# One-hots of a gather emitted a step earlier, scattered rows added one block at a time, the last turns moved ahead

## Chip, cores and metric

The kernel runs on one core of a Trainium2 chip. The time is device microseconds of one execution of the whole program; the figure compared is the median over runs. The core has five engines with queues of their own: PE (TensorE, matrix products), DVE (VectorE), ACT (ScalarE), POOL (GpSimd) and SP (SyncE, which here only issues transfers). An engine works off its own queue in order.

## What is computed

The reference is a two-layer backbone over 256 latent tokens of width 1024. Layer 0 ends in a dense SwiGLU, layer 1 in a mixture of eight experts of which each token takes two. The change touches only what follows the mixer of layer 1:

```python
h = modulate(rmsnorm(x), shift, scale)
logits = h @ moe_router                       # 256 x 8
top, idx = top2(logits); comb = softmax(top)  # two experts per token
for e in range(8):                            # E_FF = 3584
    y_e = (silu(h_e @ w1[e]) * (h_e @ w3[e])) @ w2[e]
x = x + gate * sum_e comb_e * y_e
out = rmsnorm(x) * final_norm_g
```

Every weight is float32; an expert has 3 x 14 MB, all eight have 336 MB.

## The kernel before

The program has a first part (mixers and the dense FFN, to about 820 us) and then `moe`, which fills the rest. `moe` reads the expert weights in **units** of 1 MB: an expert's 3584 hidden columns are cut in `EFF_CH` = 7 chunks, and a chunk has six units, two each of w1, w3 and w2. That is 8 x 7 x 6 = 336 units. All are issued by SP (L119) in the order in which the program takes them, into ten recycled buffers (nine called `raw`, one `mraw`); beside these, 8 halves called `first`, an `early` buffer and three buffers called `once` are filled before the experts begin. A recycled buffer is loaded again when its last reader is done.

**Heavy and light.** After routing, `by_load` ranks the experts by how many tokens chose them. Three are heavy (up to 128 tokens each), five are light (up to 64). A heavy unit is split into two parts by ACT (`CAST`, L145) and DVE (the remainder, L146), and PE does three products per tile (L176, L181, L182; twelve matmuls a unit). A light unit is used as it lies (L1157 for w1 and w3, L1184 for w2), with two 64-column halves side by side. `moe_turn` and `light_turn` transpose the hidden activations (L1117, L1170) and copy them to `G` (L1120, L1121) or `GL` (L1172) for the w2 product.

**Steps.** A step is one chunk of one expert. The list begins with `self.lead` = 4 light chunks of expert 0 and then mixes heavy and light chunks at an even rate. The order of instructions on PE, ACT and DVE in `moe` is pinned to the order in which the code is written. Small work of other kinds is hung between the units through callbacks: `aside` in `moe_first` (four places a heavy step, one behind each w1 or w3 unit), `heavy_aside` and `light_aside`. `look_ahead` splits the next planned unit.

**Gather.** `gather` forms the rows of one heavy and one light expert. `one_hot` (L1047) builds 0/1 matrices `P` and `Q` from each token's position; then for each of eight 128-column blocks of the width four matmuls (L1058, `sm <- P,H`) pick the rows, and DVE (L1062, L1064) and ACT (L1063 into `XE`, L1066 into `XL`) modulate and store them. `turned` transposes `P` and `Q` (L1073) and ACT casts them (L1074) for the way back. It is a generator that yields behind each block; `side` is the one under way, and `run(side, n)` moves it n yields on. `begin` does expert 0's gather, routing weights, `by_load`, and the gather of experts 1 and 4. Later gathers are started behind certain light steps (`more`).

**Scatter.** When an expert is done, `scatter` or `light_scatter` scales its output into two parts `Y`, and four times `put` multiplies them by the transposed one-hots (L1208, L1209) and adds the result, times the token's weight, to the residual (DVE, L1211). These generators lie in `late`; `puts()` runs them to the end.

**Router.** `last_proj.finish(t)` makes the logits of one of two token tiles; `route` then ranks both (L957 to L963), forms the combination weights with an exponential on ACT (L977), and the positions (L989 to L995). POOL does the two H2 subtractions of tile 1 (L1596).

Of the kernel before, what the change touches and what calls it, by code (L numbers as in the profile page):

```python
# [49 lines left out]
class Net:  # L50
    def __init__(self, tc, d, dump=None):
# [18 lines left out]
        self.hact, self.hpool = (1,), (1,)  # L70
# [873 lines left out]

    def route(self):
# [3 lines left out]
        lg, sel, oh1, oh2 = self.lg, T("sel"), T("oh1"), T("oh2")  # L949
        big = E.tile([128, 2, 2, 8, 8], F32, tag="P", name="big", bufs=1)  # L950
        gt, ge = (big[:, i] for i in range(2))
        selb = E.tile([128, 2, 8], BF16, name="selb")
        rank = T("rank")
        for t in range(2):
            mine = lg[:, t, :, None].to_broadcast([128, 8, 8])
            other = lg[:, t, None, :].to_broadcast([128, 8, 8])
            V.tensor_tensor(ge[:, t], other, mine, op=ALU.is_equal)  # L957
            V.tensor_tensor(ge[:, t], ge[:, t], self.low, op=ALU.mult)
            V.tensor_tensor(gt[:, t], other, mine, op=ALU.is_gt)
            V.tensor_tensor(gt[:, t], gt[:, t], ge[:, t], op=ALU.add)  # L960
            V.tensor_reduce(rank[:, t], gt[:, t], axis=AX.X, op=ALU.add)
            V.tensor_scalar(selb[:, t], rank[:, t], 1.5, None, op0=ALU.is_lt)
            V.tensor_scalar(sel[:, t], rank[:, t], 1.5, None, op0=ALU.is_lt)  # L963
# [32 lines left out]
        self.comb, self.sel, self.pos, self.tmp = comb, sel, pos, tmp  # L996
        self.dbg("pos", pos)

    def by_load(self):
# [31 lines left out]
        self.placed.append(table("combS", self.comb))  # L1031
# [18 lines left out]
    def gather(self, P, XE=None, XL=None):  # L1050
# [3 lines left out]
        for k in range(8):  # L1054
# [10 lines left out]
            if XL is not None:  # L1065
                nc.scalar.activation(XL[:, k], pg[:, o:], AF.Identity, bias=sh, scale=A)  # L1066
# [15 lines left out]
    def moe_first(self, src, XE, c, aside=lambda n: None):  # L1082
# [3 lines left out]
        for n, name in enumerate(("m_w1", "m_w3")):  # L1086
            ps = self.bank(tag="mm")
            for kh in range(2):
# [8 lines left out]
                self.look_ahead()  # L1097
                aside(2 * n + kh)
# [89 lines left out]
    def scatter(self, PT, y, cmb):  # L1188
# [24 lines left out]
    def light_scatter(self, PT, y, cmb):  # L1213
# [16 lines left out]
    def moe(self):  # L1230
# [3 lines left out]
        def tables(i):  # L1234
            tabs = (self.pos, self.sel, self.comb) if i == 0 else self.placed
            return [a[:, :2, i:i + 1] for a in tabs]

        def light(i, P):
# [4 lines left out]
            pos, sel, _ = tables(i)  # L1243
# [6 lines left out]
        def heavy(i, P):  # L1250
            pos, sel, _ = tables(i)
# [9 lines left out]
        def gather(i, j):  # L1261
# [4 lines left out]
            Q = light(j, P)  # L1266
            yield from self.gather(P[:, :, 0 if i else 128:192], XE.get(i), XE[j])
# [19 lines left out]
        run(side, 9)  # L1287
# [22 lines left out]

        def second(kind, **kw):

            while todo[kind] and todo[kind][0] in G:
# [21 lines left out]
        for m, (i, c) in enumerate(steps):  # L1335
            kind = big(i)
            if i == 0 and c == 4:
# [9 lines left out]
            def light_aside(n):  # L1347
                if n == 1:
                    turns(False)
                if n == 3 and big(after[0]):  # L1350
# [9 lines left out]
                elif n == 3 and todo[True] and not any(big(x) for x, _ in steps[m:]):  # L1360
                    i, c = todo[True][0]
                    self.plan = [(source(i)("m_w2", c, hb), 1) for hb in range(2)]
                if n == 3:
# [206 lines left out]
    def last_proj(self, l, mix, gates, A2, ss, xm, er):  # L1570

        tc, nc, sh, RA, shR = self.tc, self.nc, self.modc[:, 3, 0], self.RA, self.shR
        self.lg = self.C.tile([128, 2, 8], F32, name="lg")
# [175 lines left out]
```

## Time and profile before

| | |
|---|---|
| median of 3 runs | 1694.98 us (1692.75 to 1695.25) |
| the profiled execution, own time | 1690.82 us |
| its span in the profile | 1689.1 us |
| PE busy | 1608.9 us, 95% |
| DVE, ACT, POOL busy | 955.9, 679.7, 35.4 us |
| mean granted TensorE clock | 0.976 of full speed |
| moved by DMA | 481.55 MB, mean 285 GB/s |

The profile is of one execution. "PE busy" counts a matmul from its start to a modelled end, so that 95% is no measure of how near the engine is to its peak. A row of a timeline has a start, a length, the engine, the line, output and inputs, how many instructions were joined, and in brackets how long the engine was idle before and on what it waited. GB/s in a window is what the core's sixteen DMA engines moved, and the column before the DMA share is the clock that TensorE was granted: 1.00 is 2.4 GHz, 0.50 is 1.2 GHz.

### The profile page before, as it was taken

The numbers are of one execution on the slowest core, as the hardware profiler recorded it, in microseconds if no ns is written. First come the engines' busy times: TensorE is split into PE (matmuls) and PEld (weight loads), VectorE is DVE, ScalarE is ACT, GpSimd is POOL, SyncE is SP. The second block draws the span as 40 slices with busy tenths as digits, with TensorE's granted clock in tenths as the row PEclk, the third lists the DMA queues.
The fourth block names the chain that finished last, engine by engine and source line by source line (L and its number), as shares of the span: only waits on it lengthen the run. The fifth ranks groups of instructions, "written<-read, shape, count | busy, mean of one in ns | idle before, by whom it ended". The sixth has DMA issues, their size and how long they took to land. (4 is left out here: it accounts for less than half of the span.)

```text
span 1689.1 us, 23700 instructions
## 1 busy us (share of the span) xinstructions
PE 1608.9 (95%) x9333; PEld 1202.3 (71%) x9333; DVE 955.9 (57%) x1455; ACT 679.7 (40%) x1086; POOL 35.4 (2%) x46
## 2 busy tenths in 40 slices
PE   6999999999999999999899999999999999999986
PEld 3878799887787878999656766666676666775653
DVE  3769655567565688588314554447454454545343
ACT  4654244422222226765314434344343343533341
POOL 1000000000000030000000000000000000000000
PEclk9999999999999999999798999999999999999997
DMA  9544441535443542325898999999999999999994
GB/s 363 195 164 150 180 162 51 184 140 189 160 174 138 207 154 101 125 76 205 335 417 315 419 418 413 405 418 419 418 395 398 419 420 412 418 419 419 419 420 168
DMA packets 69030, 481.55 MB, mean 285 GB/s; under 512 B 8064, under 2 KB 8192, under 8 KB 12336
## 3 DMA queue, kind: packets, MB, share of 16 engines
q1 hardware_dynamic: 68480, 479.43, 71.5%
q8 instruction: 75, 1.23, 0.3%
q10 hardware_dynamic: 432, 0.54, 0.1%
q14 instruction: 43, 0.35, 0.1%
HBM read 478.86 MB, written 1.08 MB: 284 GB/s over the span
## 5 line engine op out<-in xcount | busy, mean ns | idle before, releaser
L146 DVE TENSOR_TENSOR s<-raw,s 128x1024 fp32r<-128x1024 f32 (+1 forms) x350 | 414.9, 1221 | 272.2 <-ACT s L145 271.6
L145 ACT CAST s<-raw 128x1024 fp32r<-128x1024 f32 (+1 forms) x350 | 355.4, 1050 | 277.6 <-PE mm L181 98.0
L176 PE MATMUL mm<-X,s 128*128 128x512 f32 (+1 forms) x672 | 247.2, 368 | 0.0
L181 PE MATMUL mm<-X,s 128*128 128x512 f32 (+1 forms) x672 | 247.0, 368 | 0.0
L182 PE MATMUL mm<-X,s 128*128 128x512 f32 (+1 forms) x672 | 245.8, 368 | 0.0
L1157 PE MATMUL mm<-raw,XL 128*64 128x256 f32 x1952 | 218.9, 380 | 0.6 <-DMA raw<-in_m_w_dram 0.6
L1157 PEld LDWEIGHTS mm<-raw,XL 128*64 128x64 f32 x1952 | 138.7, 137 | 82.6 <-issue 15.9
L176 PEld LDWEIGHTS mm<-X,s 128*128 128x128 f32 x672 | 126.4, 188 | 27.9 <-issue 6.7
L181 PEld LDWEIGHTS mm<-X,s 128*128 128x128 f32 x672 | 126.7, 189 | 26.0 <-issue 5.9
L182 PEld LDWEIGHTS mm<-X,s 128*128 128x128 f32 x672 | 126.6, 189 | 24.0 <-issue 3.4
L176 PE MATMUL mm<-s,XE 128*128 128x512 f32 x336 | 139.2, 414 | 2.2 <-ACT s L145 2.1
L181 PE MATMUL mm<-s,XE 128*128 128x512 f32 x336 | 136.4, 406 | 2.0 <-DVE s L146 2.0
L182 PE MATMUL mm<-s,XE 128*128 128x512 f32 x336 | 135.9, 404 | 0.0
L1184 PE MATMUL yl<-raw,GL 128*64 128x512 f32 x488 | 110.5, 597 | 0.5 <-ACT GL L1172 0.5
L1161 ACT ACTIVATE t<-mm 128x256 f32<-128x256 f32 x35 | 13.5, 386 | 218.9 <-PE mm L1157 218.9
L176 PE MATMUL mm<-s,X 128*128 128x256 f32 (+1 forms) x304 | 86.5, 287 | 2.0 <-ACT mix L666 2.0
L181 PE MATMUL mm<-s,X 128*128 128x256 f32 (+1 forms) x304 | 86.0, 285 | 0.8 <-DVE s L146 0.8
L1163 DVE TENSOR_TENSOR t<-t,mm 128x256 f32<-128x256 f32 x35 | 14.6, 417 | 125.0 <-PE mm L1157 124.9
L182 PE MATMUL mm<-s,X 128*128 128x256 f32 (+1 forms) x304 | 85.1, 285 | 0.0
L1184 PEld LDWEIGHTS yl<-raw,GL 128*64 128x64 f32 x488 | 33.0, 137 | 63.6 <-issue 62.0
L176 PEld LDWEIGHTS mm<-s,XE 128*128 128x128 f32 x336 | 65.6, 195 | 17.3 <-ACT s L145 3.1
L181 PEld LDWEIGHTS mm<-s,XE 128*128 128x128 f32 x336 | 65.5, 195 | 17.4 <-DVE s L146 3.1
(384 smaller groups left out, 2347.7 us busy)
## 6 DMA issues: line engine op xcount, KB each, us to landing
raw<-in_m_w_dram SPq DMA_DIRECT2D x294, 1024.0 KB, 14.0
mraw<-in_mod_w_dram SPq DMA_DIRECT2D x47, 1024.0 KB, 4.9
raw<-in_f_w_dram SPq DMA_DIRECT2D x33, 1024.0 KB, 5.0
mraw<-in_m_w_dram SPq DMA_DIRECT2D x32, 1024.0 KB, 12.4
raw<-in_w_in_dram SPq DMA_DIRECT2D x20, 1024.0 KB, 4.8
raw<-in_w_out_dram SPq DMA_DIRECT2D x8, 1024.0 KB, 5.6
first<-in_m_w_dram SPq DMA_DIRECT2D x8, 512.0 KB, 9.0
once<-in_m_w_dram SPq DMA_DIRECT2D x3, 1024.0 KB, 16.1
```

The source lines that it names most:

```text
L145: self.last = (nc.scalar.copy(s1[:, :h], r), nc.vector.tensor_tensor(s2[:, :h], r, s1[:, :h].bitcast(F32), op=ALU.subtract))
L146: nc.vector.tensor_tensor(s2[:, :h], r, s1[:, :h].bitcast(F32), op=ALU.subtract))
L176: m = mm(out, a[0], b[0], start=first, stop=False)
L181: self.keep(mm(out, a[0], b[1], start=False, stop=False))
L182: self.keep(mm(out, a[1], b[0], start=False, stop=last))
L1157: self.keep(nc.tensor.matmul(ps[64 * b:64 * b + 64], XL[:, k], w(o, o + 256), start=(k == 0), stop=(k == 7), tile_position=(0, 64 * b)))
L1161: nc.scalar.activation(g, ps, AF.Silu)
L1163: self.keep(nc.vector.tensor_tensor(g, g, ps, op=ALU.mult))
L1184: self.keep(self.nc.tensor.matmul(y[64 * hf:64 * hf + 64], G[:, b, 64 * hb:64 * hb + 64], w(o, o + 512), start=(c == 0 and hb == b == 0), ...
```

## The change

1. **Ranks by tile.** `rank_of(t)` is called in `finish(t)`, so tile 0 is ranked before tile 1's logits exist. The H2 subtractions of tile 1 move from POOL to DVE (`hpool` empty).
2. **Weights later.** `weights()` and the third table `combS` leave `begin` for the start of step (0,1). In expert 0's gather every second block is stored by DVE in place of ACT.
3. **First heavy gather in pieces.** The gather of experts 1 and 4 runs three blocks at a time within the second, third and fourth lead steps.
4. **One-hots a step ahead.** `gather` yields once more, after its one-hots, and they are emitted as soon as the gather is started.
5. **One put at a time.** `put()` moves the oldest scatter on by one block per heavy aside; scatters yield behind each block.
6. **Aside before look_ahead** in three of the four places of `moe_first`.
7. **The end.** Behind the last heavy step, `light_aside` turns the heavy rows and does the pending puts between w1 and w3 of the last light step, where before the turn stood behind that step's products and the puts behind its end.

On SP's queue two things move besides: the third load into a `once` buffer, issued before the register loads of `by_load` (L1022) in the old order, stands behind them and behind one `mraw` and one `raw` load in the new one.

```diff
+    def rank_of(self, t):
+        nc, V, lg = self.nc, self.nc.vector, self.lg
...
+        V.tensor_reduce(self.rank[:, t], gt, axis=AX.X, op=ALU.add)
+        V.tensor_scalar(self.selb[:, t], self.rank[:, t], 1.5, None, op0=ALU.is_lt)
+        V.tensor_scalar(self.sel[:, t], self.rank[:, t], 1.5, None, op0=ALU.is_lt)
...
-        self.hact, self.hpool = (1,), (1,)
+        self.hact, self.hpool = (1,), ()
...
             if XL is not None:
-                nc.scalar.activation(XL[:, k], pg[:, o:], AF.Identity, bias=sh, scale=A)
+                if o == 0 and k % 2:
+                    nc.vector.tensor_scalar(XL[:, k], pg, A, sh, op0=ALU.mult, op1=ALU.add)
+                else:
+                    nc.scalar.activation(XL[:, k], pg[:, o:], AF.Identity, bias=sh, scale=A)
             yield
...
-                self.look_ahead()
-                aside(2 * n + kh)
+                if 2 * n + kh == 1:
+                    self.look_ahead()
+                    aside(1)
+                else:
+                    aside(2 * n + kh)
+                    self.look_ahead()
...
                 self.put(t, s, PT[:, t], Y1[:, s], Y2[:, s], cmb)
+                yield
...
             Q = light(j, P)
+            yield
             yield from self.gather(P[:, :, 0 if i else 128:192], XE.get(i), XE[j])
...
             yield from gather(None, 0)
-            self.weights()
             self.by_load()
-            yield
             yield from gather(1, NH + 1)
...
-        run(side, 9)
+        run(side, 10)
...
+        def put():
+            if late and next(late[0], self) is self:
+                late.pop(0)
...
         def heavy_aside(n):
             if n == 1:
                 turns(False)
-                puts()
+                put()
                 second(True, aside=lambda: run(side, 1))
-            elif n == 3:
-                puts()
+            else:
+                put()
             run(side, 1)
...
+            if i == 0 and c == 1:
+                self.weights()
+                self.combS = self.table("combS", self.comb)
...
-            def light_aside(n):
-                if n == 1:
+            def light_aside(k):
+                if k == 1:
                     turns(False)
-                if n == 3 and big(after[0]):
+                    if not any(big(x) for x, _ in steps[m:]):
+                        turns(True)
+                        puts()
+                    if 0 < m < n:
+                        run(side, 3)
+                if k == 3 and big(after[0]):
...
             if not kind and todo[True] and not any(big(x) for x, _ in steps[m:]):
-                turns(True)
                 second(True, aside=lambda: turns(False))
             if (i, c) in more:
                 puts()
                 run(side)
                 side = gather(*more[i, c])
+                run(side, 1)
```

Three places show how the queues change. The line numbers of the changed kernel differ: L1157 becomes L1164, L1170 L1177, L1184 L1191, L1211 L1219, L1120 L1127, L1121 L1128, L1161 L1168, L1163 L1170, L1172 L1179, L1241 and L1242 (the memsets of `P` and `Q`) L1253 and L1254.

**PE, lead steps of expert 0.** Before, the end of the fourth lead step (L1157 are its last w3 units) and the first gather blocks of experts 1 and 4:

```order
L1170 MATMUL sm_7631<-ident,t_1235_7540 128x128 x2
L1157 MATMUL mm_7637<-raw_7638,XL_7203 64x256 x8
L1157 MATMUL mm_7637<-raw_7648,XL_7203 64x256 x8
L1058 MATMUL sm_7672<-P_7658,H_6724 128x192 x2
L1058 MATMUL sm_7672<-P_7658,H_6725 128x192 x2
L1058 MATMUL sm_7682<-P_7658,H_6724 128x192 x2
L1058 MATMUL sm_7682<-P_7658,H_6725 128x192 x2
L1058 MATMUL sm_7692<-P_7658,H_6724 128x192 x2
```

After, the second lead step: three of these blocks stand behind its w1 units.

```order
L1164 MATMUL mm_7437<-early,XL_7206 64x256 x8
L1164 MATMUL mm_7437<-raw_7446,XL_7206 64x256 x8
L1177 MATMUL sm_7456<-ident,t_1221_7381 128x128 x2
L1058 MATMUL sm_7461<-P_7367,H_6727 128x192 x2
L1058 MATMUL sm_7461<-P_7367,H_6728 128x192 x2
L1058 MATMUL sm_7471<-P_7367,H_6727 128x192 x2
L1058 MATMUL sm_7471<-P_7367,H_6728 128x192 x2
L1058 MATMUL sm_7481<-P_7367,H_6727 128x192 x2
L1058 MATMUL sm_7481<-P_7367,H_6728 128x192 x2
L1164 MATMUL mm_7492<-raw_7493,XL_7206 64x256 x8
L1164 MATMUL mm_7492<-raw_7503,XL_7206 64x256 x8
L1191 MATMUL yl_7514<-raw_7515,GL_7459 64x512 x4
```

The gather has left its place behind the lead steps for three places within them, each behind a light turn (L1177).

**DVE, a light expert's scatter in a heavy step.** Before, two split units (L146) and then all four additions to the residual `res`:

```order
L146 TENSOR_TENSOR s_1440_8450<-raw_8447,s_1439_8449 128x1024
L146 TENSOR_TENSOR s_1442_8454<-raw_8447,s_1441_8453 128x1024
L146 TENSOR_TENSOR s_1445_8473<-raw_8470,s_1444_8472 128x1024
L146 TENSOR_TENSOR s_1447_8477<-raw_8470,s_1446_8476 128x1024
L1211 SCALAR_TENSOR_TENSOR res_1968<-mm_8485,comb,res_1968 128x512
L1211 SCALAR_TENSOR_TENSOR res_1968<-mm_8489,comb,res_1968 128x512
L1211 SCALAR_TENSOR_TENSOR res_1969<-mm_8493,comb,res_1969 128x512
L1211 SCALAR_TENSOR_TENSOR res_1969<-mm_8497,comb,res_1969 128x512
```

After, the four additions, here called L1219, stand singly between the split units (rows of the stretch from the first to the last of them):

```order
L1128 TENSOR_TENSOR G_1439_8433<-sm_8427,G_1438_8432 128x512
L1219 SCALAR_TENSOR_TENSOR res_1968<-mm_8450,comb,res_1968 128x512
L146 TENSOR_TENSOR s_1445_8457<-raw_8454,s_1444_8456 128x1024
L146 TENSOR_TENSOR s_1447_8461<-raw_8454,s_1446_8460 128x1024
L146 TENSOR_TENSOR s_1450_8480<-raw_8477,s_1449_8479 128x1024
L146 TENSOR_TENSOR s_1452_8484<-raw_8477,s_1451_8483 128x1024
L1219 SCALAR_TENSOR_TENSOR res_1968<-mm_8492,comb,res_1968 128x512
L146 TENSOR_TENSOR s_1458_8511<-raw_8508,s_1457_8510 128x1024
L146 TENSOR_TENSOR s_1460_8515<-raw_8508,s_1459_8514 128x1024
L146 TENSOR_TENSOR s_1463_8533<-raw_8530,s_1462_8532 128x1024
L146 TENSOR_TENSOR s_1465_8537<-raw_8530,s_1464_8536 128x1024
L1219 SCALAR_TENSOR_TENSOR res_1969<-mm_8553,comb,res_1969 128x512
```

Between one addition and the next there are now the splits of two units (four L146). The same engine's one-hots of the next gather (`P`, `Q`), before:

```order
L1121 TENSOR_TENSOR G_1489_8667<-sm_8661,G_1488_8666 128x512
L146 TENSOR_TENSOR s_1494_8687<-raw_8684,s_1493_8686 128x1024
L146 TENSOR_TENSOR s_1496_8691<-raw_8684,s_1495_8690 128x1024
L1047 TENSOR_SCALAR P_8694<-iot,posS,selS 128x128 x2
L1241 MEMSET P_8694 128x2x64
L1242 MEMSET Q_8699 128x2x64
L1047 TENSOR_SCALAR P_8694<-iot,posS,selS 128x64 x2
```

and after:

```order
L1170 TENSOR_TENSOR t_1474_8599<-t_1474_8599,mm_8622 128x256
L1047 TENSOR_SCALAR P_8664<-iot,posS,selS 128x128 x2
L1253 MEMSET P_8664 128x2x64
L1254 MEMSET Q_8669 128x2x64
L1047 TENSOR_SCALAR P_8664<-iot,posS,selS 128x64 x2
L1047 TENSOR_SCALAR Q_8669<-iot,posS,selS 128x64 x2
L1128 TENSOR_TENSOR G_1499_8684<-sm_8678,G_1498_8683 128x512
L1062 TENSOR_SCALAR t_1503_8706<-sm_8701,A_1099_6660,modc_3101 128x128
```

The one-hots have passed the two split rows of one unit and the remainder of `G` (L1121, now L1128).

**ACT, the last heavy chunk's w2.** Before, its four casts (two units, L145) and then the copy to `G`:

```order
L1161 ACTIVATE t_2446_12961<-mm_12962 128x256
L145 CAST s_2454_13007<-raw_13005 128x1024
L145 CAST s_2456_13011<-raw_13005 128x1024
L145 CAST s_2459_13017<-mraw_13015 128x1024
L145 CAST s_2461_13021<-mraw_13015 128x1024
L1120 CAST G_2464_13031<-sm_13026 128x512
L1172 COPY GL_13050<-sm_13047 128x256
```

After:

```order
L1127 CAST G_2455_12991<-sm_12986 128x512
L1168 ACTIVATE t_2450_12964<-mm_12965 128x256
L145 CAST s_2461_13019<-raw_13017 128x1024
L145 CAST s_2463_13023<-raw_13017 128x1024
L145 CAST s_2466_13029<-mraw_13027 128x1024
L145 CAST s_2468_13033<-mraw_13027 128x1024
L1179 COPY GL_13053<-sm_13050 128x256
```

The copy to `G` has passed the four casts and the silu of the light step (L1161, now L1168).

## Rows read from the trace of the kernel before

**Rows 1.** The page's busy shares.

```profile
PE 1608.9 (95%) x9333; PEld 1202.3 (71%) x9333; DVE 955.9 (57%) x1455; ACT 679.7 (40%) x1086; POOL 35.4 (2%) x46
```

**Rows 2.** Windows: each engine's busy us, PEclk, DMA share, GB/s.

```profile
889.00:921.00 32.00, 29.37 (x152) 18.25 (x152) 12.90 (x15) 13.42 (x20) 0.00 (x0) 0.86 0.75 280
921.00:1662.00 741.00, 705.63 (x4056) 479.98 (x4054) 364.41 (x415) 299.16 (x395) 0.00 (x0) 0.98 1.01 414
```

**Rows 3.** Timeline of PE, 820 to 838: start, length, instructions, idle before.

```profile
823.30 4.47 PE L1058 MATMUL sm<-P,H 128*128 128x64 f32 x20 [0.74 <-ACT XL L1066]
828.63 9.28 PE L1157 MATMUL mm<-first,XL 128*64 128x256 f32 x64
```

**Rows 4.** Timelines of DVE, POOL and ACT at the routing.

```profile
816.52 1.03 DVE L962 TENSOR_SCALAR selb<-rank 128x8 bf16<-128x8 f32 x1
817.47 0.16 DVE L963 TENSOR_SCALAR sel<-rank 128x8 f32<-128x8 f32 x1
...
816.26 2.49 POOL L1596 TENSOR_TENSOR H<-t,H 128x512 fp32r<-128x512 f32 x2 [1.45 <-ACT t L1592]
...
821.46 1.28 ACT L977 ACT_TABLE_LOAD   x1
```

**Rows 5.** Timeline of PE, 876 to 902.

```profile
876.31 3.67 PE L1157 MATMUL mm<-raw,XL 128*64 128x256 f32 x32
...
884.18 4.76 PE L1058 MATMUL sm<-P,H 128*128 128x192 f32 x16 [0.45 <-ACT XL L1066]
...
892.97 0.79 PE L176 MATMUL mm<-s,XE 128*128 128x512 f32 x1 [1.62 <-ACT s L145]
...
899.01 0.39 PE L182 MATMUL mm<-s,XE 128*128 128x512 f32 x1
...
901.11 0.39 PE L182 MATMUL mm<-s,XE 128*128 128x512 f32 x1
```

**Rows 6.** Timelines of ACT and DVE, the first heavy split units.

```profile
891.87 1.99 ACT L145 CAST s<-raw 128x1024 fp32r<-128x1024 f32 x2
...
892.95 2.36 DVE L146 TENSOR_TENSOR s<-raw,s 128x1024 fp32r<-128x1024 f32 x2 [2.73 <-ACT s L145]
```

**Rows 7.** Waits, 921 to 1662: us in total, times, longest.

```profile
PE mm L1208 <- DVE res L1211: 12.2, 4, 3.1
...
PE sm L1058 <- DVE P L1047: 9.7, 3, 3.4
...
PE y L176 <- ACT G L1120: 5.0, 1, 5.0
...
PE sm L1073 <- ACT XL L1066: 4.6, 2, 2.3
```

**Rows 8.** Windows at one of these waits, and behind another.

```profile
990.00:1000.00 10.00, 6.94 (x25) 5.18 (x24) 6.09 (x8) 3.79 (x5) 0.00 (x0) 0.84 1.01 419
...
1090.00:1100.00 10.00, 10.00 (x64) 4.45 (x62) 0.49 (x1) 0.00 (x0) 0.00 (x0) 1.00 0.95 356
```

**Rows 9.** Timeline of DVE, a light scatter's additions.

```profile
992.64 2.36 DVE L146 TENSOR_TENSOR s<-raw,s 128x1024 fp32r<-128x1024 f32 x2 [1.89 <-ACT s L145]
994.91 2.72 DVE L1211 SCALAR_TENSOR_TENSOR res<-mm,comb,res 128x512 f32<-128x512 f32 x4
```

**Rows 10.** Timelines of PE and ACT at the end; a window.

```profile
1638.48 1.95 PE L1157 MATMUL mm<-raw,XL 128*64 128x256 f32 x16 [0.55 <-DMA raw<-in_m_w_dram]
...
1646.02 0.79 PE L176 MATMUL y<-s,G 128*128 128x512 f32 x1 [5.01 <-ACT G L1120]
...
1658.90 7.08 PE L1157 MATMUL mm<-raw,XL 128*64 128x256 f32 x64
...
1668.90 3.65 PE L1184 MATMUL yl<-raw,GL 128*64 128x512 f32 x16 [0.46 <-ACT GL L1172]
...
1643.49 1.99 ACT L145 CAST s<-mraw 128x1024 fp32r<-128x1024 f32 x2 [0.50 <-DMA mraw<-in_m_w_dram]
...
1662.00:1663.00 1.00, 1.00 (x12) 0.65 (x10) 0.00 (x0) 0.38 (x1) 0.00 (x0) 1.00 0.20 78
```

More of the change, by code (lines that the diff above doesn't have):

```diff
@@ L942, in ffn @@
         second(DFF_CH - 1, prev)
+    def rank_of(self, t):
+        nc, V, lg = self.nc, self.nc.vector, self.lg
+        gt, ge = (self.t2((128, 8, 8), tag="t1") for _ in range(2))
+        mine = lg[:, t, :, None].to_broadcast([128, 8, 8])
+        other = lg[:, t, None, :].to_broadcast([128, 8, 8])
+        V.tensor_tensor(ge, other, mine, op=ALU.is_equal)
+        V.tensor_tensor(ge, ge, self.low, op=ALU.mult)
+        V.tensor_tensor(gt, other, mine, op=ALU.is_gt)
+        V.tensor_tensor(gt, gt, ge, op=ALU.add)
+        V.tensor_reduce(self.rank[:, t], gt, axis=AX.X, op=ALU.add)
+        V.tensor_scalar(self.selb[:, t], self.rank[:, t], 1.5, None, op0=ALU.is_lt)
+        V.tensor_scalar(self.sel[:, t], self.rank[:, t], 1.5, None, op0=ALU.is_lt)
     def route(self):
@@ L948, in route @@
         T = lambda nm, *sh: E.tile([128, 2, 8, *sh], F32, name=nm)
[L949 to L963, printed above, removed]
+        lg, sel, selb, rank, oh1, oh2 = self.lg, self.sel, self.selb, self.rank, T("oh1"), T("oh2")
         m = E.tile([128, 4, 2], F32, name="mx")
@@ L995, in route @@
         V.tensor_copy(pos, pp)
-        self.comb, self.sel, self.pos, self.tmp = comb, sel, pos, tmp
+        self.comb, self.pos, self.tmp = comb, pos, tmp
         self.dbg("pos", pos)
@@ L1030, in by_load @@
         self.placed = [table(*a) for a in (("posS", self.pos[:, :2]), ("selS", self.sel))]
-        self.placed.append(table("combS", self.comb))
+        self.table = table
         self.slots, over, overi = T("slots", 2, 8), T("over", 1), E.tile([128, 1], I32, name="overi")
@@ L1234, in tables, with one_hots @@
         def tables(i):
-            tabs = (self.pos, self.sel, self.comb) if i == 0 else self.placed
+            tabs = (self.pos, self.sel, self.comb) if i == 0 else self.placed + [self.combS]
             return [a[:, :2, i:i + 1] for a in tabs]
+        def one_hots(i):
+            return [a[:, :2, i:i + 1] for a in ((self.pos, self.sel) if i == 0 else self.placed)]
         def light(i, P):
@@ L1242, in light @@
             nc.vector.memset(Q[:, :, :64].bitcast(F32), 0.0)
-            pos, sel, _ = tables(i)
+            pos, sel = one_hots(i)
             self.one_hot(P[:, :, 128:192], pos, sel)
@@ L1250, in heavy @@
         def heavy(i, P):
-            pos, sel, _ = tables(i)
+            pos, sel = one_hots(i)
             self.one_hot(P[:, :, :128], pos, sel)
@@ L1266, in gather @@
             Q = light(j, P)
+            yield
             yield from self.gather(P[:, :, 0 if i else 128:192], XE.get(i), XE[j])
@@ L1359, in light_aside @@
                         self.plan[2:2] = [(source(i)("m_w2", c, hb), 1) for hb in range(2)]
-                elif n == 3 and todo[True] and not any(big(x) for x, _ in steps[m:]):
+                elif k == 3 and todo[True] and not any(big(x) for x, _ in steps[m:]):
                     i, c = todo[True][0]
                     self.plan = [(source(i)("m_w2", c, hb), 1) for hb in range(2)]
-                if n == 3:
+                if k == 3:
                     for _ in range(2):
@@ L1572, in last_proj @@
         tc, nc, sh, RA, shR = self.tc, self.nc, self.modc[:, 3, 0], self.RA, self.shR
-        self.lg = self.C.tile([128, 2, 8], F32, name="lg")
+        self.lg, self.rank, self.sel = (self.C.tile([128, 2, 8], F32, name=n) for n in ("lg", "rank", "sel"))
+        self.selb = self.C.tile([128, 2, 8], BF16, name="selb")
         lgp = [self.bank((128, 8), tag="sm") for _ in range(2)]
```

2 lines of the change are left out of this document (added).

## Prediction

> **What bounds the kernel now.** The page comes first: PE is busy for 95% of the span [rows 1], which says little, since the share is a mean over stages. So the windows are read by stretch, the GB/s column before the others. While nothing holds it, the weight stream moves 419 GB/s, in a window in which PE waits too (the first of [rows 8]); a unit of 1,048,576 bytes takes 2.50 us at this pace, 336 units 841 us. That is half of the time, and no part of the change makes it less. What can be had is what the stream loses, and what PE does after it has ended. The stream loses 32 x (1 - 280/419) = 10.6 us in 889 to 921, and 741 x (1 - 414/419) = 8.8 us from there to 1662 [rows 2]. It has ended by 1663 (78 GB/s in the last window of [rows 10], nothing behind it), and PE starts the last w2 product only at 1668.90. So I read the kernel as one stream that is held back when PE frees buffers too late, and a tail behind it.
>
> **The start.** Three edits meet here.
> The first `selb` takes 1.03 us on DVE while POOL works on H2; `sel`, the same operation into another type, takes 0.16 [rows 4]. With the POOL work gone I expect 0.9 back on it, and as much on tile 1's; the exponential's table load (1.28, [rows 4]), behind which PE waits 0.74 for `XL` [rows 3], leaves this stretch too. Against this stand two subtractions of 512 columns on DVE. DVE does 1024 columns in 2.36/2 = 1.18 [rows 6], so 512 are some 0.6 each. That is -2 x 0.9 - 0.74 + 1.2 = -1.3; the ranks of tile 0 also lie beside the logits of tile 1, and I take 1.6, with 0.7 and 2.5 as ends. The first expert matmul moves from 828.63 [rows 3] to 827.0.
> The Trainium skill, in "SBUF — State Buffer", section "SBUF: two separate sides", says that VectorE and GpSimd share one pair of ports, held as an exclusive lock for a whole instruction. The 1.03 against 0.16 us agrees; whether it is the port or only the output type no row tells.
> On SP the third `once` load falls behind a `mraw` and a `raw` load, which wait for buffers that PE frees. One unit fewer is then in store when PE starts: 2.50 us lost, 1.6 won, so the stream stands **0.9 us later** there (ends: 2.5 later, 2.5 earlier if the load had no room anyway).
> The gather of experts 1 and 4 leaves the place behind the lead steps. There PE takes no unit from 879.98 (876.31 + 3.67) to 892.97, 13.0 us, and its wait of 1.62 for the first split follows it [rows 5]. Meanwhile the buffers fill, and that is the stall of 10.6. Spread over three lead steps, the same blocks cost PE at most 4.76/4 = 1.19 each [rows 5], 3.6 a step. A lead step has six units of 3.67/2 = 1.84 us; 6 x 1.84 + 3.6 = 14.6 us is 2.44 a unit, still under 2.50, so the stream hides the blocks. And the first heavy units are split (ACT 1.99, DVE 2.36, [rows 6]) while the last lead step still runs. What is late next: a heavy unit takes PE 12 x (901.11 - 899.01)/9 = 2.8 us [rows 5], more than 2.50, so the full buffers hold the stream a little still. I take 2.0 us for it (0 if the lead was eaten, 4.6 if PE also waits for the first split). The start gives 10.6 - 2.0 - 0.9 = **7.7 us** (3.5 to 13).
>
> **The middle.** Waits of PE from 921 on [rows 7]: 12.2 us in four for a light scatter's additions, 9.7 in three for one-hots, 4.6 in two for the last `XL` of a gather, 5.0 in one at the end. The reason for the first is seen in [rows 9]: four additions (2.72) stand behind two splits (2.36) that began at 992.64, and PE needs the bank of the first addition. The order shows both chains undone: additions singly between units, one-hots a unit earlier. So 21.9 us of waits go. Each such wait also brings a lower clock: the window 990 to 1000 has 0.84 [rows 8], which is 3.2 us at 0.50, 1.6 us of work lost; seven times 1.6 is 11.2. PE's stretch of 741 us becomes 741 - 33.1 = 708. I add 0.5 us of new waiting at each of the 24 gather blocks (three gathers of eight), where the first of a block's stores can come behind an addition of 2.72/4 = 0.68; the bounds are 0 and the 2.3 that a wait for `XL` takes now. That is 12 us, so 720. The stream needs 741 - 8.8 = 732 for its units. PE is then no longer the slower of the two on the mean, and what remains are the two waits for `XL`, which the order leaves: behind one of them the stream does 356 instead of 419 [rows 8], 1.5 us lost; with the other and a little more I leave 1.8 of the 8.8. The middle gives **7.0 us** (2 to 8.8). That the waits total 22 us and I count 7 is the point: the stream ran at 419 in the window of the wait itself, and buffers hide the rest.
>
> **The end.** ACT's copy to `G` stands behind four casts, the last two of which wait for a load, to 1643.49 [rows 10]; so PE idles 5.01 and begins the last heavy w2 product at 1646.02, and at the lower clock (its first matmul takes 0.79, against 0.39 in [rows 5]); the product ends where the two light units ahead of 1658.90 begin, at 1658.90 - 3.65 = 1655.3. With the copy ahead of the casts PE can start one cast (1.99/2) behind 1641.0 (1643.49 less one unit's 2.50), at about 1642.1. Its second unit is split from 1643.49 on, with 2.36 of DVE behind the first cast of 1.0: 1646.9; six matmuls of 0.233 later, at some 1648.5, it is done, 6.8 earlier. Two light units (3.65) and four (7.08), the additions that now lie between them (four, about 2.2, which before lay just as much on the path to 1668.90) and the turn follow: the last product starts at 1662.0 to 1662.7. By then its weights are there, the stream having ended by 1663 [rows 10]. I take **6.2 us** (2 to 8.3; the upper end if the additions hide in waits for loads).
>
> **Sum.** 7.7 + 7.0 + 6.2 = 20.9. The profiled execution, 1690.82 (span 1689.1 and 1.7 around it), would become 1669.9. It lies 4.2 under the median of 1694.98, so the median to expect is 1694.98 - 20.9 = **1674.1**. Weights and `combS` moved into step (0,1) cost nothing, as DVE and ACT idle most of the lead steps; the cover goes if PE waits there, at about 1 us.
>
> **The rivals.** From here a difference under 0.2%, 3.4 us, counts as no change, for a measurement of this kernel hardly tells it.
> (a) *The middle gives nothing.* The waits for `XL` and the new small waits keep PE late where buffers are already full; -13.9, **1681.1**. For it: 8.8 is small against 35 us of idle PE, so most was hidden, and what isn't could be those two. Against: they are 2 of 9.
> (b) *The start gives nothing.* The lead bursts find PE with less in store and the heavy start is held as before; -13.2, **1681.8**. Against: 2.44 under 2.50, but by little.
> (c) *The tail gives nothing, as the clock falls.* When PE has caught up, it works 1.84 of each 2.50 us and waits 0.7. If each wait brought the lower clock, a light unit would take 1.84 + 1.6 = 3.4 us, 0.9 over the pace; eight units, 7.5 us, which eats the 6.2: **1681.6**. [Rows 10] speak against it: behind the wait of 0.55 at 1638.48, 16 matmuls take 1.95, the full clock's time; in [rows 8] it took a wait of some 3.
> The Trainium skill's "TensorE: Matmul & The Clock Gate", section "HAM oscillation — how this bites in real kernels", tells of such a loop: compute shorter than the wait for data, so that each tile starts at the lower clock. It speaks against this change; by it the time would be that of (c), or more if it held in the middle too.
> (d) *No change.* The stream's own pace was the limit where I read stalls, and the tail is held by landings: within 3.4 us of **1695**.
> (e) *Slower.* Stores of a gather block and an addition stand ahead of the next unit's splits on DVE, and PE starves for splits. DVE then has 2.36 + 0.68 per unit and L1062 and L1064, of 128 columns each, which I put at 0.4 apiece at most (an addition of 512 takes 0.68): 3.8 us. PE has 2.8, four matmuls of the gather (at most 1.19) and two of the addition (2 x 0.23): 4.5. So DVE keeps up, with little to spare. At a wait w at each of 24 blocks PE needs 708 + 24w. From w = 1.0 the stream is late (732); from w = (741 + 13.9 - 708)/24 = 1.95 all gains of start and end are eaten. At the price of a present wait for `XL`, 2.3 and 1.6 of clock, it is 708 + 94 = 802, 61 over 741: **1742**.
>
> **How the numbers follow.** Forecast 0.56, with a range of its own of 1668 to 1681; (a) 0.13, (b) 0.09, (c) 0.08, (d) 0.06, (e) 0.08. Faster is all but (d) and (e): 0.86; same 0.06; slower 0.08. The range 1667 to 1684 takes in the forecast's and (a) to (c) with their bounds, and leaves out (d), (e) and the best corner (13 + 8.8 + 8.3 gives 1665).
>
> **What would show it.** Start: three groups of L1058 in the lead steps, no gap before the first heavy unit, over 400 GB/s in the 32 us around it. Middle: no wait of PE for `res` or `P` above 1 us; two for `XL` left; 418 or more from there to the end. End: no 5 us wait for `G`, the last w2 product beginning within a microsecond of the last load. It is wrong if PE waits for `s` at the gather blocks, if the clock column falls in light steps, or if the stream loses at a new place what it gains at 889.

## The result, and the profile after

The changed kernel takes 1674.47 us (1671.40 to 1674.81, four runs) against 1694.24 before (1692.75 to 1695.25, four runs): the ratio is 0.9887, with a 95% interval of 0.9875 to 0.9899. The medians lie 19.8 us apart; the forecast was 1674.1. The profiled execution took 1674.13, with a span of 1672.4.

The windows of the changed kernel answer to [rows 2]; the last one is the end of the weight stream.

```profile
841.00:889.00 48.00, 45.49 (x331) 25.86 (x328) 9.49 (x25) 15.46 (x33) 0.00 (x0) 1.00 0.94 373
889.00:921.00 32.00, 32.00 (x179) 21.19 (x178) 15.66 (x16) 12.76 (x17) 0.00 (x0) 1.00 1.01 422
921.00:1645.00 724.00, 694.44 (x4022) 467.55 (x4020) 359.64 (x412) 293.53 (x385) 0.00 (x0) 0.99 1.01 420
1640.00:1650.00 10.00, 10.00 (x74) 5.74 (x72) 3.60 (x6) 1.00 (x2) 0.00 (x0) 1.00 0.72 293
```

The hole of 280 GB/s around the first heavy unit is closed, and from there on the stream runs at 420 without a break. A new loss stands in the lead steps: 373 GB/s in 841 to 889. The clock column of these four rows stands at 0.99 or above; what that says of rival (c) follows below.

PE in the lead steps and at the first heavy unit, and SP over the same stretch:

```profile
864.40 1.90 PE L1164 MATMUL mm<-once,XL 128*64 128x256 f32 x16
866.13 1.90 PE L1164 MATMUL mm<-mraw,XL 128*64 128x256 f32 x16
...
868.15 1.45 PE L1058 MATMUL sm<-P,H 128*128 128x192 f32 x8
...
871.84 3.67 PE L1164 MATMUL mm<-raw,XL 128*64 128x256 f32 x32
...
884.76 3.67 PE L1164 MATMUL mm<-raw,XL 128*64 128x256 f32 x32
888.37 0.50 PE L176 MATMUL mm<-s,XE 128*128 128x512 f32 x1
```

```profile
841.91 0.42 SPq L107 DMA_DIRECT2D once<-in_m_w_dram  x1
846.18 15.35 SPq L119 DMA_DIRECT2D raw<-in_m_w_dram  x8
868.07 0.34 SPq L119 DMA_DIRECT2D mraw<-in_m_w_dram  x1
873.83 15.45 SPq L119 DMA_DIRECT2D raw<-in_m_w_dram  x9
```

The first heavy matmul follows the last light one with no wait, where it waited 1.62 in [rows 5]. But SP gets `mraw` back only at 868.07, when PE is done with it, and the next `raw` at 873.83: between the two lie the third group of L1058 and the turns, 868.15 to 871.84. Ahead of it PE worked off `once` units, which are never loaded again and so free nothing.

PE's waits from 921 on, to be read against [rows 7]:

```profile
PE mm L181 <- DVE s L146: 7.6, 10, 0.8
PE mm L176 <- ACT s L145: 5.2, 6, 1.1
PE sm L1058 <- DVE P L1047: 4.7, 3, 2.1
PE sm L1076 <- ACT XL L1069: 3.6, 2, 1.8
PE mm L1164 <- DMA raw<-in_m_w_dram: 1.8, 5, 0.5
```

The waits for `res` have gone (12.2), those for one-hots are halved (9.7 to 4.7). Sixteen short waits for splits of w1 and w3 make 12.8 us, where before three made 2.0. They lie at ten heavy units, and at each of the ten ACT's cast had itself waited 2.6 to 4.5 us for the weights to land, as here ahead of the wait at 1309.48:

```profile
1308.38 1.99 ACT L145 CAST s<-raw 128x1024 fp32r<-128x1024 f32 x2 [4.48 <-DMA raw<-in_m_w_dram]
```

So these are waits for the stream, seen through the split: PE has caught up with it.

The end, PE and then ACT, beside [rows 10]:

```profile
1629.72 0.49 PE L176 MATMUL y<-s,G 128*128 128x512 f32 x1 [0.85 <-ACT s L145]
1630.98 0.50 PE L181 MATMUL y<-s,G 128*128 128x512 f32 x1 [0.77 <-DVE s L146]
...
1634.94 0.44 PE L1177 MATMUL sm<-ident,t 128*128 128x128 f32 x2 [1.12 <-DVE t L1170]
...
1635.44 0.40 PE L181 MATMUL y<-s,G 128*128 128x512 f32 x1
...
1638.11 3.65 PE L1191 MATMUL yl<-raw,GL 128*64 128x512 f32 x16
...
1652.56 3.65 PE L1191 MATMUL yl<-raw,GL 128*64 128x512 f32 x16 [0.46 <-ACT GL L1179]
```

```profile
1625.30 0.58 ACT L1127 CAST G<-sm 128x512 fp32r<-128x512 f32 x1 [15.60 <-PE sm L1124]
1625.78 0.39 ACT L1168 ACTIVATE t<-mm 128x256 f32<-128x256 f32 x1
1628.62 1.99 ACT L145 CAST s<-raw 128x1024 fp32r<-128x1024 f32 x2 [2.45 <-DMA raw<-in_m_w_dram]
```

`G` is cast 2.7 us before its weights land (1625.88 against 1628.62). PE begins one cast behind the landing, and its matmuls take the full clock's 0.40.

**A ledger of the stream.** To split the gain I summed GB/s times length over windows of 5 us (longer ones further on), with time counted for each kernel from the end of the router's last logits matmul (814.85 before, 818.13 after) and the sum begun 30 us ahead of it, and turned the difference in 1 MB units into time, at 2.50 us each. This is how far each profiled execution's stream is ahead of that of before, so many us behind the logits:

```
behind logits, us      50     75    110    400    820
changed kernel       +0.4   -3.5   +7.3  +10.4  +17.4
gather_late          +2.7   +0.8   +3.7   +6.9  +14.0
gather_134            0.0   -5.9   +4.7   +8.0  +15.2
gather_3302          -1.3   -2.7   +6.4   +9.6  +16.7
gather_2204          -1.0   -2.3   +6.9  +10.2  +17.3
once_2               -1.2   -3.9   +6.9  +10.1  +17.2
ranks_old            -3.9   -8.0   +2.7   +5.9  +13.0
puts_bulk            -0.9   -4.6   +6.0   +9.3  +16.4
hots_late            +0.7   -3.3   +7.3  +10.6  +17.7
ahead_first          +0.7   -3.4   +7.3  +10.4  +17.4
mid_old              +0.5   -3.5   +7.2   +8.2   +8.8
tail_old             -0.5   -4.3   +6.3   +9.5  +16.7
tail_only            +0.5   +0.5   +0.8   +0.9   +1.6
```

Each row is one execution, and most of the difference between alike ones arises in the first 50 us: `gather_3302`, `puts_bulk`, `hots_late`, `ahead_first`, `mid_old` and `tail_old` do the same work there as the changed kernel, and stand between -1.3 and +0.7. From 50 to 110 us, the last five of these, which have the changed kernel's lead steps, gain 6.6 to 6.9, and that kernel 6.9.

In the changed kernel the start gives 7.3 us, the middle 10.1. From the logits to the end of the program it takes 1672.4 - 818.13 = 854.3, before 1689.1 - 814.85 = 874.2: 19.9 us in all, so 2.5 are left for the end.

### The profile page after: what moved, and what is told of

Its sections match the earlier page's. It is cut to its first block, busy times and chain, and to the rows that moved or that the text cites. A ratio compares the mean times of both kernels' runs of the same rounds, so it can differ in the third digit from the quotient of the medians.

```text
span 1672.4 us, 23690 instructions
## 1 busy us (share of the span) xinstructions
PE 1601.2 (96%) x9333; PEld 1193.3 (71%) x9333; DVE 958.6 (57%) x1465; ACT 677.5 (41%) x1078; POOL 32.9 (2%) x44
## 3 DMA queue, kind: packets, MB, share of 16 engines
HBM read 478.86 MB, written 1.08 MB: 287 GB/s over the span
## 5 line engine op out<-in xcount | busy, mean ns | idle before, releaser
L146 DVE TENSOR_TENSOR s<-raw,s 128x1024 fp32r<-128x1024 f32 (+1 forms) x350 | 414.3, 1221 | 270.5 <-ACT s L145 268.7
L145 ACT CAST s<-raw 128x1024 fp32r<-128x1024 f32 (+1 forms) x350 | 354.9, 1050 | 272.0 <-PE mm L181 97.2
L176 PE MATMUL mm<-X,s 128*128 128x512 f32 (+1 forms) x672 | 247.1, 368 | 0.0
L181 PE MATMUL mm<-X,s 128*128 128x512 f32 (+1 forms) x672 | 247.0, 368 | 0.0
L1164 PE MATMUL mm<-raw,XL 128*64 128x256 f32 x1952 | 219.9, 380 | 1.8 <-DMA raw<-in_m_w_dram 1.8
L1164 PEld LDWEIGHTS mm<-raw,XL 128*64 128x64 f32 x1952 | 138.7, 137 | 84.3 <-issue 16.3
L176 PEld LDWEIGHTS mm<-X,s 128*128 128x128 f32 x672 | 126.4, 188 | 27.9 <-issue 6.7
L181 PEld LDWEIGHTS mm<-X,s 128*128 128x128 f32 x672 | 126.7, 188 | 26.0 <-issue 5.9
L176 PE MATMUL mm<-s,XE 128*128 128x512 f32 x336 | 137.3, 409 | 5.6 <-ACT s L145 5.2
L181 PE MATMUL mm<-s,XE 128*128 128x512 f32 x336 | 135.4, 403 | 7.6 <-DVE s L146 7.6
L182 PE MATMUL mm<-s,XE 128*128 128x512 f32 x336 | 134.5, 400 | 0.0
L1191 PE MATMUL yl<-raw,GL 128*64 128x512 f32 x488 | 110.5, 597 | 0.5 <-ACT GL L1179 0.5
L1168 ACT ACTIVATE t<-mm 128x256 f32<-128x256 f32 x35 | 13.5, 386 | 204.7 <-PE mm L1164 204.6
L176 PE MATMUL mm<-s,X 128*128 128x256 f32 (+1 forms) x304 | 87.2, 289 | 1.9 <-ACT mix L666 1.9
L181 PE MATMUL mm<-s,X 128*128 128x256 f32 (+1 forms) x304 | 86.7, 287 | 0.8 <-DVE s L146 0.8
L181 PEld LDWEIGHTS mm<-s,XE 128*128 128x128 f32 x336 | 64.3, 191 | 24.7 <-DVE s L146 10.7
L176 PEld LDWEIGHTS mm<-s,XE 128*128 128x128 f32 x336 | 64.3, 191 | 22.1 <-ACT s L145 8.0
L1191 PEld LDWEIGHTS yl<-raw,GL 128*64 128x64 f32 x488 | 33.0, 137 | 63.6 <-issue 62.4
L182 PEld LDWEIGHTS mm<-s,XE 128*128 128x128 f32 x336 | 64.0, 191 | 15.1
```

Source lines behind the costliest of these rows:

```text
L145: self.last = (nc.scalar.copy(s1[:, :h], r), nc.vector.tensor_tensor(s2[:, :h], r, s1[:, :h].bitcast(F32), op=ALU.subtract))
L146: nc.vector.tensor_tensor(s2[:, :h], r, s1[:, :h].bitcast(F32), op=ALU.subtract))
L176: m = mm(out, a[0], b[0], start=first, stop=False)
L181: self.keep(mm(out, a[0], b[1], start=False, stop=False))
L182: self.keep(mm(out, a[1], b[0], start=False, stop=last))
L1164: self.keep(nc.tensor.matmul(ps[64 * b:64 * b + 64], XL[:, k], w(o, o + 256), start=(k == 0), stop=(k == 7), tile_position=(0, 64 * b)))
```

## The experiments

My theory was the forecast's: the stream was held at three places, each by the wait named there. The main rivals: the start comes from the routing; the waits of the middle were hidden; the end is held by landings.

### The first gather back behind the lead steps (gather_late)

```diff
-                    if 0 < m < n:
-                        run(side, 3)
```

> The changed kernel with the gather of experts 1 and 4 back in one piece behind the lead steps. If that placement is what took away the stall before the first heavy unit, the stall of about 10 us returns, the small loss of 3.5 us within the lead steps goes, and the time rises by 7 to 11 us, to 1682 to 1685. If the start was gained by the ranks and the routing instead, the time stays within 2 us of the changed kernel's 1674.5.

Measured: 1676.77 us, ratio 0.9906 (0.9891 to 0.9921), some 3 us slower than the changed kernel's 0.9887; the two intervals still touch. From the logits to the end it takes 857.4 us (1675.7 - 818.33) against 854.3. The stall is back, the lead steps are whole:

```profile
841.00:889.00 48.00, 45.36 (x322) 25.62 (x318) 6.32 (x20) 10.36 (x25) 0.00 (x0) 0.98 1.00 407
889.00:921.00 32.00, 29.30 (x155) 18.15 (x155) 13.37 (x15) 13.93 (x20) 0.00 (x0) 0.88 0.77 291
```

The mechanism is right, the price was not: 7 to 11 was expected. In the ledger this kernel is 4.3 ahead of the changed one at 75 us and 3.6 behind it at 110. From 75 to 110 the changed kernel gains 10.8 us and this one 2.9; of that difference of 7.9 the changed kernel had paid 4.3 beforehand. The undoing is not of the spread alone: SP issues all three `once` loads early again (817.19, three in a row), and 2.3 of the 4.3 stand at 50 us already.

### Additions in bulk (puts_bulk), one-hots late (hots_late), look_ahead first (ahead_first)

```diff
         def heavy_aside(n):
             if n == 1:
                 turns(False)
-                put()
+                puts()
                 second(True, aside=lambda: run(side, 1))
-            else:
-                put()
+            elif n == 3:
+                puts()
             run(side, 1)
```

> The changed kernel with all four additions of a scatter made together again, at the second or fourth aside. PE then waits again for the additions, four times 3 us plus 1.6 us of lower clock each. If these waits held the weight stream, 3 to 6 us of the 10 us that the stream gained behind 921 go, and the time is 1677 to 1680. If buffers hide them, so that the gain came from the one-hots, it stays within 1 us of 1674.5.

```diff
             Q = light(j, P)
-            yield
+            if early:
+                yield
...
                 side = gather(*more[i, c])
-                run(side, 1)
```

(`early` is true in `begin` alone.)

> The changed kernel with the later gathers' one-hots emitted together with their first block again. PE waits again three times about 3 us for P, each followed by a lower clock. If these waits held the stream, the time rises by 3 to 5 us, to 1677 to 1680; if they were hidden, it stays within 1 us of 1674.5. Together with the run on the additions: if neither alone costs anything, the stream was lost only where both came close together.

```diff
-                if 2 * n + kh == 1:
-                    self.look_ahead()
-                    aside(1)
-                else:
-                    aside(2 * n + kh)
-                    self.look_ahead()
+                self.look_ahead()
+                aside(2 * n + kh)
```

> The changed kernel with look_ahead in front of the aside again in all four places, so that on ACT and DVE a gather block's stores and an addition stand behind the next unit's split. If that order matters, the stores come 2 to 3 us later, PE waits at the gather blocks and the time rises by 1 to 3 us, to 1675.5 to 1677.5. If it is the slower rival's place that hurts (stores ahead of splits starve PE), the time falls below 1674. Otherwise no difference beyond 1 us.

Measured: 1672.96, 1673.62 and 1673.51 us, ratios 0.9883, 0.9885 and 0.9883, all inside the changed kernel's interval. None of the three costs anything that is seen alone, though the long waits for the additions are all back in the first:

```profile
PE mm L1216 <- DVE res L1219: 12.2, 4, 3.1
```

By itself this would say that my middle term was wrong, and that the waits were hidden. So all three were undone at once.

### All three together (mid_old)

> The changed kernel with the three edits of the middle undone together: additions in bulk, one-hots with their first block, look_ahead ahead of every aside. Each alone cost nothing. If they stand in for one another (three long waits come close together at each gather, and the buffers can take two of them but not three), the stream loses its 10 us behind 921 again and the time is about 1683. If the middle was gained by the earlier start alone, it stays at 1673.5 to 1674.5.

Measured: 1681.81 us (1674.70 to 1683.84, six runs), ratio 0.9932 (0.9916 to 0.9948): 7 to 8 us slower than the changed kernel. One of the six runs, at 1674.70, was as fast as the changed kernel; no trace of it was kept, and why stays open. In the trace its waits are those of before, and so is its stream behind 921:

```profile
PE mm L1212 <- DVE res L1215: 12.2, 4, 3.1
PE sm L1058 <- DVE P L1047: 9.8, 3, 3.4
PE sm L1076 <- ACT XL L1069: 4.6, 2, 2.3
```

```profile
921.00:1645.00 724.00, 690.90 (x3973) 470.25 (x3973) 356.66 (x408) 293.18 (x384) 0.00 (x0) 0.98 1.01 416
```

By the ledger 8.6 us go, nearly all of the middle's 10.1. In windows of 10 us the stream falls to between 306 and 399 GB/s in seven, all at a gather or close to one (from 1080, 1090, 1190, 1220, 1230, 1270 and 1410 on); the changed kernel, `puts_bulk` and `hots_late` have none under 412 up to 1640. So the edits stand in for one another. That the ten buffers take a part of the waits that come close together, and not all, is my reading; no run had another number of recycled buffers. Which pair of the three is enough wasn't run.

### The old end on the new kernel (tail_old), the new end on the old (tail_only)

```diff
                 if k == 1:
                     turns(False)
-                    if not any(big(x) for x, _ in steps[m:]):
-                        turns(True)
-                        puts()
...
             if not kind and todo[True] and not any(big(x) for x, _ in steps[m:]):
+                turns(True)
                 second(True, aside=lambda: turns(False))
```

> The changed kernel with the old end: the heavy rows turned behind the last light products, the additions behind everything. By the forecast's term the end is worth 6.2 us, so 1680.7; by the stream's ledger in the two traces only 2.4 us are left for it, so 1677; if the end is held by landings alone, 1674.5.

> The kernel before with only the new end. By the forecast's term 6.2 us faster than before, 1688; by the ledger of the two traces 2.4 us, 1692; by the path from the landing of the last heavy unit to the last product (27.9 us before, 24.0 after) 3.9 us, 1690.4.

`tail_only` is the same edit, the other way round, on the kernel before. Measured: 1677.15 us, ratio 0.9909 (0.9894 to 0.9924), so 3.7 us slower than the changed kernel by the ratios; and 1688.15, ratio 0.9977 (0.9967 to 0.9987), 3.9 faster than before. By the medians the end is worth 4 us on either kernel. By the single traces, from the logits to the end, it is more: 860.0 us in `tail_old` (1675.4 - 815.40), 5.7 longer than the changed kernel, and 868.3 in `tail_only` (1686.8 - 818.55), 6.0 shorter than before; 0.7 and 1.6 of these are the stream's by the ledger, which leaves 5.0 and 4.4. PE's timeline of `tail_old` has the old wait at the old size:

```profile
1631.95 0.80 PE L176 MATMUL y<-s,G 128*128 128x512 f32 x1 [5.01 <-ACT G L1127]
...
1655.65 3.65 PE L1191 MATMUL yl<-raw,GL 128*64 128x512 f32 x16 [0.46 <-ACT GL L1179]
```

### Where the blocks of the first gather lie (gather_134, gather_3302, gather_2204), and the once load (once_2)

```diff
-                        run(side, 3)
+                        run(side, (0, 1, 3, 5)[m])
```

> The changed kernel with one, three and four blocks of the first gather in the three lead steps instead of three, three and two. In the changed kernel the stream loses 4 us around 868, where SP waits for the mraw buffer until PE has worked off three once units, which free nothing. If it is PE's lateness from the early blocks, two blocks fewer ahead of that place (about 1.7 us) give 1 to 2 us back: 1672.5 to 1673.5. If it is the late issue of the third once load, nothing changes. If the later burst stalls the stream at the first heavy unit, it is slower by 1 to 2 us.

```diff
-        self.gstep, self.gfrom, self.nonce, self.opos = 1, 1, 3, 10
+        self.gstep, self.gfrom, self.nonce, self.opos = 1, 1, 2, 10
```

> The changed kernel with two once buffers instead of three, so that no once load stands behind mraw and raw on SP. If the place of the third load on SP caused the loss around 868, this is up to 4 us faster, 1670.5 to 1674. If the loss comes from PE's lateness, one unit fewer is in store and one more must go through the recycled buffers: no better, up to 2.5 us slower, 1674.5 to 1677.

Measured: 1677.73, ratio 0.9911 (0.9896 to 0.9926), and 1673.71, ratio 0.9888. Fewer early blocks made it some 4 us slower, so that theory of mine fell: SP in `gather_134` gets `mraw` back earlier, at 866.14, but the next `raw` only at 876.46, for the third burst is now the long one. Without the third `once` buffer the time is the same at the end, and the lead steps still lose 2.7 (-1.2 to -3.9), so the place of that load is not what stalls them; what the place costs by itself this run can't say, for it has a buffer less. The next idea was to take the third burst out of the lead steps:

```diff
-                    if 0 < m < n:
+                    if m in (1, 2, 4):
                         run(side, 3)
```

> The changed kernel with the last two blocks and the turns of the first gather one step later, in the light step ahead of the first heavy one; the third lead step is free of them. With one, three and four blocks the loss around 868 had grown, so what counts is not the number of early blocks but the burst between the release of mraw and that of the next raw buffer, 3.7 us of PE (868.15 to 871.84). Without it the release comes 3.7 us earlier: the stream gains 2 to 3.5 us, and the time is 1671 to 1672.5. If the buffers are short at the first heavy unit instead, the burst is paid there: no gain, 1674.5, or up to 2 us slower.

> As gather_3302, but with two, two and four blocks. Less PE time ahead of the release (about 1.7 us), more ahead of the first heavy unit. If the release alone counts, as fast as gather_3302 or 1 us faster; if the first heavy unit is the tighter place, 1 to 3 us slower than it.

(`gather_2204` has `(0, 2, 2, 0, 5)[m]` in place of the 3.) Measured: 1670.88 (1669.42 to 1674.45), ratio 0.9871 (0.9857 to 0.9886), and 1673.20, ratio 0.9885. The intervals overlap that of the changed kernel, and from the logits to the end the profiled executions take 854.5 and 854.6 us against 854.3: no gain is shown. In `gather_3302` SP gets the next `raw` 2.3 us behind `mraw` (869.60, 871.85), where it took 5.8, but its nine `raw` loads then take 20.14 us in place of 15.45. Counted from 50 us, the two kernels gain 7.7 and 7.9 up to 110 against 6.9: most of the burst is paid later, and 1 us at most is won, which these times can't tell from nothing.

### The router as it was (ranks_old)

The edit puts `rank_of` for both tiles back into `route`, `hpool` to `(1,)`, `weights()` and `combS` into `begin`, and takes out the alternation of `XL`. The two temporaries come from another pool than before.

> The changed kernel with the router as it was: both tiles ranked together, the H2 subtractions of tile 1 on POOL, the weights and their table in begin, every block of expert 0 stored by ACT. The span from the router's last logits matmul is the measure (854.3 us in the changed kernel). In the traces the first expert matmul came 2.0 us earlier after those logits; the three other parts undone cost 3.1, 5.7 and 7.2 of the 20.0 us by which this stretch became shorter, which leaves 4. If the router's part is what is left, the stretch takes 856 to 858; if its 2 us are taken up by full buffers at the first heavy unit, 854.3 to 855.

Measured: 1676.52 us, ratio 0.9902 (0.9885 to 0.9918), some 2.5 us slower than the changed kernel by the ratios, whose intervals overlap; by the measure named beforehand 1674.8 - 816.29 = 858.5, which is 4.2 more than 854.3 and a little beyond the 856 to 858. So in single traces the four groups, undone one at a time, cost 3.1, 7.2, 5.7 and 4.2, together 20.2 of the 19.9. This is no clean undoing. Its temporaries make DVE wait for POOL, which neither kernel does there:

```profile
820.28 0.17 DVE L1255 MEMSET P<- 128x128 f32 x1 [3.12 <-POOL H L1623]
```

Its first expert matmul comes 14.2 us behind the logits, against 13.8 before and 11.8 after, and its stream is 1.2 us back at the logits already. So 2.5 and 4.2 are both upper bounds for the router's part.

## Why the prediction was right

**What bounds it** held: a stream with holes and a tail. At 420 GB/s over 724 us no hole is left behind 921, and PE now waits for landings. The rivals that let the middle (a) or the start (b) give nothing, or all of it (d), fell by the ledger's 10.1 and 7.3. But the total hides three wrong parts, and that it came within 0.4 us is luck: the middle gave 3.1 more than forecast, and the end added 3.7 less.

**The start**, 7.7 forecast, 7.3 by the ledger; here too errors cancelled. The routing was forecast at 1.6 and gave 2.0 to the first matmul (13.8 to 11.8 us behind the logits). The step that a lead step "is 2.44 a unit, still under 2.50, so the stream hides the blocks" failed: the mean over a step left out that the units in `once` free nothing, and that a burst delays the one buffer that SP waits for in order; the stream lost 3.9 us there (from +0.4 to -3.5). Against this the step "the full buffers hold the stream a little still", 2.0, fell away: the hole of 10.6 closed wholly (10.8). The stream also stood 0.4 ahead at 50 us, where 0.9 behind was forecast. The `once` load was taken at 2.5; `gather_late`, where it keeps its old place, is 2.3 ahead at 50 us, in single executions.

`selb` now takes 0.17 us with the same output type as in [rows 4], so it was not the type that made it 1.03:

```profile
817.32 0.17 DVE L956 TENSOR_SCALAR selb<-rank 128x8 bf16<-128x8 f32 x1
```

In `tail_only`, which has the old router, it takes 1.03 again, beside POOL's two subtractions:

```profile
819.97 2.49 POOL L1598 TENSOR_TENSOR H<-t,H 128x512 fp32r<-128x512 f32 x2 [1.44 <-ACT t L1594]
```

```profile
820.23 1.03 DVE L962 TENSOR_SCALAR selb<-rank 128x8 bf16<-128x8 f32 x1
```

That agrees with the Trainium skill's "SBUF — State Buffer", section "SBUF: two separate sides", on the shared ports. No run has the new code with POOL beside `selb`: in `ranks_old` POOL does the subtractions again, but DVE waits for them, and `selb` runs behind them at 0.17.

**The middle**, 7.0 forecast, was 10.1: I left 1.8 for the two waits for `XL`, which stay (3.6 us) but hold the stream no more, and took the stream's pace as 419 where it is 420 to 422. New waiting was put at 12 us, at the 24 gather blocks. There, between the first and the last block of each gather, PE waits for no split of w1 or w3; the 12.8 us in L176 and L181 lie elsewhere and have another cause, the stream, so that 12 and 12.8 are alike by chance. The step that failed besides is "one-hots a unit earlier", with no wait above 1 us: three waits stay, 2.1, 1.6 and 1.0. The stream shows no loss at them. What the forecast did not see is that the edits are redundant; it added their waits up as if each held the stream.

**The end**, 6.2 forecast, is worth 4 by the medians of two runs, 4.4 to 5.0 by their traces. The failing step is "six matmuls of 0.233 later, at some 1648.5, it is done", which is 7.5 us behind the landing of the product's first unit: it took 9.5 (1628.62 to 1638.11). Between its two units the light step's turn (L1177) stands in PE's queue and waits 1.12 for L1170, which stands behind four splits on DVE; so all twelve matmuls of the second unit come behind the splits, where I had six left. Of what the end is worth the total keeps 2.5 by the ledger, since the stream's finish is now uneven: by bytes it is 17.4 us ahead, but the first unit of the last heavy w2 lands 15.7 ahead (1641.00 - 814.85 against 1628.62 - 818.13), and the last bytes come at 293 GB/s over ten us. From that landing to the last product it is 27.9 us before and 23.9 after; 15.7 and 4.0 make up the 19.9 but for 0.2.

**The rivals.** Slower (e) failed on its place and its price: it needed 1.95 us at each of 24 gather blocks, and within the gathers PE waits only three times for a split, each time of w2, for 0.2 to 0.5 us. (c) failed on the clock: it is 0.99 over the 724 us, and waits of 0.85 and 1.12 at the end are followed by matmuls at full speed. Once, behind three waits for data (0.26 to 0.45) and two for splits (1.08, 0.76) from 1585 on, it did fall, and it falls behind the waits of 2.1 and 1.6 for `P` (0.69 in 1020 to 1025, 0.66 in 1380 to 1385):

```profile
1595.00:1600.00 5.00, 4.38 (x12) 3.47 (x13) 4.87 (x6) 3.81 (x6) 0.00 (x0) 0.66 1.01 421
```

The loop in the Trainium skill's "TensorE: Matmul & The Clock Gate", section "HAM oscillation — how this bites in real kernels", computes for less time than it waits for data. In (c) 1.84 us of work stand against 0.7 of waiting, so the prediction read that section too widely: it does not give (c)'s time, and this kernel does not test it.

**The signs.** Of those named, the three groups in the lead steps, 422 GB/s around the first heavy unit, 420 behind it, the two waits for `XL` and the missing wait for `G` came. Two did not: the waits for `P` above 1 us, and a last w2 product within a microsecond of the last load; it begins at 1652.56, when the stream has been done for 1.6 to 2.6 us (25 GB/s in 1650 to 1651, none behind it). Of the signs of being wrong, a loss at a new place came in part, 3.9 us against the 10.8 gained.

## What to carry to other kernels

Where a stream with buffers feeds the work, count what the stream loses, window by window, not what the engines wait; then undo edits together as well as singly, for waits that stand in for each other look free one by one. A burst of other work is hidden only if no buffer that the queue waits for in order is held behind it, and units in buffers that are never refilled give the queue nothing to go on with. Moving such a burst from one tight place to another, ahead of the same slower stage, may move the loss and not the time: here the release came 3.5 us sooner behind `mraw`, and no gain is shown.

## What the runs showed of the hardware

The first part of the program has two courses that no edit explains. In four of the fourteen profiled executions, the one before among them, TensorE's clock in 20 to 30 us is 0.83 to 0.97, and the first write of `grow` is issued at 114.3 to 114.8. In the other ten, the changed kernel's and that of `tail_only`, which is the old program there, the clock is 0.50 to 0.54, and that write comes at 117.3 to 118.1. What follows is shifted by these 3 us. The first line is the kernel before, the second the changed one:

```profile
20.00:30.00 10.00, 7.75 (x94) 4.38 (x86) 5.34 (x17) 5.14 (x11) 0.00 (x0) 0.97 1.01 419
```

```profile
20.00:30.00 10.00, 9.51 (x69) 4.40 (x62) 4.38 (x14) 3.45 (x8) 0.00 (x0) 0.51 1.01 420
```

A single execution of this kernel thus carries 3 us that belong to neither version, which is why the ledger counts from the logits.
